# An encoder block on one core: casts of the inverse operands moved ahead in the gates stage, projection stores one step later

## The chip, the cores and the metric

The kernel runs on one core of a Trainium2 chip. The metric is the device time of one execution in microseconds (us); less is better. The engines of a core work side by side, each through its own queue of instructions in the order in which they were written into it: PE (matrix products; its weight loads are listed as PEld), DVE (vector), ACT (scalar and activation), POOL, and SP, which here only issues DMA transfers. An instruction that waits holds up everything behind it on its engine.

## The reference

One layer of a bidirectional encoder block on x of 2048 x 1024 float32. Cut to what matters here:

```
proj = rms_norm(x) @ w_in                                  # 2048 x 3600
cv   = short_conv3(proj[:, :2560])                         # q, k, hv, hx1, hx2
q, k = silu(cv[q]), silu(cv[k]) / sqrt(128);  v, o = proj  # o through a sigmoid
h_m  = mlstm(q, k, v, gates) + flipped mlstm
z    = hx1 * two_sided_fft_conv(hv, filters 0)
z    = hx2 * two_sided_fft_conv(z,  filters 1)
x    = x + rms_norm(concat(norm(h_m * o), norm(z)) @ w_out)
x    = x + rms_norm(square(relu(rms_norm(x) @ w1)) @ w2)
```

The convolution by FFT over 4096 points is done as matrix products in two stages each way: a first forward stage, a second forward stage whose spectrum is multiplied by the filter's, a second inverse stage and a first inverse stage.

## The kernel before

Products in higher precision are made of three: an operand is split into a high part (a cast by `act.copy`, line 166) and a low part (a subtraction, line 169), and `mm3` (lines 154 to 161) multiplies low by high, high by low and high by high into one bank.

The kernel goes through these stages: normalise x; the filters' spectra; the convolution operator `hyena`; the mLSTM; output projection; MLP. The input projection is no stage of its own. It is a generator, `project`, whose pieces `drive` (line 217) lays between those of the filters and of `hyena`: each `yield` of either names a cost, and the projection gets a next piece whenever the cost of the other side is ahead. First come the `convolved` columns (20 tiles of 128 columns, each in four blocks of 512 rows): a block has three pieces, in which `block` makes the products, `centre` and `sides` the width-3 convolution, `turn` the transposes of an earlier block (for all but q and k), `gated` the Silu (for q and k), and `stored` copies the transposes out of their bank (line 626) and stores them by two DMAs of POOL's queue (line 630), or stores q and k by SP's. `ahead` prepares the next column tile's weights: a product on POOL, a cast on ACT, a subtraction on DVE. Then comes `values_project`: four groups of about 260 columns in the order 3, 0, 1, 2, 16 tiles of 128 rows each, in two half steps of 12 products. `outputs` writes a tile from its bank to half of a buffer `vst` (lines 706 and 708; the sigmoid is the o gate), and after the second tile of a pair `stored` issues one store by SP to the tensor `vo`. There are two `vst` buffers and four banks.

From the start of `hyena` the order of all queues is the order in which the code is written out (`manual_schedule`), so a line that is moved moves in every queue.

`hyena` (line 1005) has the first forward stage of hv (16 turns), the second stages with filter 0 (a loop over 32 values of j), then **the gates stage** (lines 1156 to 1190) and the second stages with filter 1. The gates stage has 17 turns h. A turn makes the first inverse products `py` of row tile h from two operands, multiplies them by the gate tile (line 1181) to z, splits z, and makes from z of turn h - 1 the first forward products of the second convolution: `first` (line 1043), two times three products into banks of their own with a `yield` behind each, and then a copy of the first bank by ACT (line 1051), of the second by DVE (line 1052) and a store of the pair by ACT's queue. It splits the two operands of turn h + 1 (`operand`, line 1163: high part on ACT, low part of the first on POOL and of the second on DVE) and issues the three loads of turn h + 2. High parts have four buffers, raw tiles six, z and its low part four between them, products three banks.

Of the kernel before, what the change touches and what calls it, by code (L numbers as in the profile page):

```python
# [8 lines left out]
F32 = mybir.dt.float32  # L9
# [138 lines left out]
class Builder:  # L148
# [410 lines left out]
    def convolved(self, cts, then):  # L559

        wk, hn, cw = self.pw, self.hn, self.cw
        pe, dve, act, pool = self.pe, self.dve, self.act, self.pool
        n = 4 * len(cts)
        fetched, weights, pts, ys, sts = {}, {}, {}, {}, {}

        def ahead(c, step):

            if c >= len(cts):
                next(then)
                return  # L570
            fetch, chunk, m = self.in_weights(128 * cts[c], 128)
            if step == 0:
                fetched[c] = [fetch(q) for q in range(m)]
            else:
                weights.setdefault(c, []).append(chunk(fetched[c][step - 1]))

        def of(i):
            return cts[i // 4], i % 4

        def block(i, ks):  # L580
            ct, b = of(i)
            if ks[0] == 0:
                pts[i] = self.pp.tile([128, 512], F32, tag="pp", name="pt")
            for k in ks:
                self.mm3(pts[i], self.row_block(weights[i // 4], k), (hn[b][0][:, k, :], hn[b][1][:, k, :]), k == 0, k == 7)

        def centre(i):
            ct, b = of(i)
            yc = ys[i] = wk.tile([128, 512], F32, tag="yc", name="yc", bufs=4)
            act.activation(yc, pts[i], AF.Identity, scale=cw[:, ct, 1:2], bias=cw[:, ct, 3:4])  # L590

        def sides(i):
            (ct, b), pt, yc = of(i), pts[i], ys[i]

            def add(y, at, p, src, w):
                dve.scalar_tensor_tensor(y[:, at], p[:, src], cw[:, ct, w:w + 1], y[:, at], ALU.mult, ALU.add)

            if b > 0:

                add(ys[i - 1], slice(511, 512), pt, slice(0, 1), 2)  # L600
                add(yc, slice(0, 1), pts.pop(i - 1), slice(511, 512), 0)
            add(yc, slice(1, 512), pt, slice(0, 511), 0)
            add(yc, slice(0, 511), pt, slice(1, 512), 2)
            if b == 3:
                pts.pop(i)

        def gated(i):
            if of(i)[0] < 8:
                act.activation(ys[i], ys[i], AF.Silu)

        def turn(i):
            ct, b = of(i)
            if ct < 8:
                return
            pt = sts[i] = self.pp.tile([128, 4, 128], F32, tag="ptt", name="ptt", bufs=1)
            for q in range(4):
                pe.transpose(pt[:, q, :], ys[i][:, 128 * q:128 * q + 128], self.eye)

        def stored(i):
            (ct, b), yc = of(i), ys.pop(i)  # L620
            if ct < 8:
                self.load(self.qk[ct // 4][ct % 4][:, 512 * b:512 * b + 512], yc)
                return
            which, cc = (ct - 8) // 4, 128 * (ct % 4)
            st = wk.tile([128, 520], F32, tag="vst", name="vst")[:, 0:512].rearrange("p (q c) -> p q c", q=4)
            act.copy(st, sts.pop(i))  # L626

            dst = self.vp[which].rearrange("h (b a) c -> (h b) a c", a=32)
            for e in range(2):
                pool.dma_start(dst[:, 8 * b + e:8 * b + 8:2, cc:cc + 128], st[64 * e:64 * e + 64])  # L630

        for step in range(3):
            ahead(0, step)
        for i in range(n + 3):
            live, b = i < n, i % 4
            if live:
                block(i, range(0, 3))
            if 1 <= i <= n:
                centre(i - 1)
            if i >= 3:  # L640
                turn(i - 3)
            if live and b == 1:
                ahead(i // 4 + 1, 0)
            yield 2.04 if live else next(then)
            if live:
                block(i, range(3, 6))
            if 1 <= i <= n:
                sides(i - 1)
            if i >= 3:
                stored(i - 3)  # L650
            if live and b > 1:
                ahead(i // 4 + 1, b - 1)
            yield 2.04 if live else next(then)
            if live:
                block(i, range(6, 8))
            if 2 <= i <= n + 1:
                gated(i - 2)
            yield 1.36 if i < n - 1 else 1.36 * live + next(then)

    def values_project(self):  # L660

        wk, act, dve, N = self.pw, self.act, self.dve, 260
        raws, chunks, pts, sts = {}, {}, {}, {}
# [9 lines left out]
        order = (3, 0, 1, 2)  # L673
# [25 lines left out]
        def outputs(g, t):  # L699
            pt, n = pts.pop((g, t)), width(g)  # L700
            if t % 2 == 0:
                sts[g] = wk.tile([128, 520], F32, tag="vst", name="vst").rearrange("p (u c) -> p u c", u=2)
            st = sts[g][:, t % 2]
            nv = 0 if g > 1 else N - 8 if g == 1 else N
            if nv:
                dve.tensor_copy(st[:, 0:nv], pt[:, 0:nv])
            if nv < n:
                act.activation(st[:, nv:n], pt[:, nv:n], AF.Sigmoid)
            if g == 3:

                for d in range(2):
                    c0 = 8 * d
                    dve.tensor_tensor(self.gin[:, :, 64 * d + (15 - t if d else t):64 * d + 64:16],
                                      pt[:, n + c0:n + c0 + 8].rearrange("p (k h) -> p k h", k=2),
                                      bg[:, c0:c0 + 8].rearrange("p (k h) -> p k h", k=2), ALU.add)

        def stored(g, t):
            if t % 2:
                n = width(g)
                self.load(self.vo[128 * t - 128:128 * t + 128, N * g:N * g + n].rearrange("(u p) c -> p u c", p=128),  # L720
                          sts[g][:, :, 0:n])

        last, steps = None, [(g, t) for g in order for t in range(16)]
        for i, (g, t) in enumerate(steps):
            block(g, t, range(0, 4))
            if last:
                outputs(*last)
            yield 1.4
            block(g, t, range(4, 8))
            if last:  # L730
                stored(*last)
            last = g, t
            yield 1.4
            nxt = steps[min(i + 7, len(steps) - 1)][0]
            if nxt != g and t in (9, 11):
                fetch(nxt, t // 11)
            if nxt != g and t == 15:
                for q in range(2):
                    chunk(nxt, q)
                    fetch(nxt, q + 2)  # L740
                yield 4.0
                for q in range(2, 4):
                    chunk(nxt, q)
            if i >= 18 and i % 2 == 0:
                next(gates, None)
        outputs(*last)
        stored(*last)
        for _ in gates:
            pass
# [255 lines left out]
    def hyena(self, pools):  # L1005
        nc, io, tc, dt = self.nc, self.io, self.tc, self.dt
        pe, dve, act, pool = self.pe, self.dve, self.act, self.pool
        wk, ps = pools
# [8 lines left out]
        def parts(raw, low=None, eng=pool):  # L1017

            hi = wk.tile([128, 512], F32R, tag="hi", name="hi", bufs=4)
            low = raw if low is None else low  # L1020
            self.split(hi, low, raw.bitcast(F32), eng)
            return hi, low
# [17 lines left out]
        def short(dtype=F32):  # L1040
            return wk.tile([128, 512], dtype, tag="z", name="z", bufs=4)
# [26 lines left out]
        for o in range(2):  # L1068
# [94 lines left out]
            def operand(h, r):  # L1163
                if h < 16:
                    y.setdefault(h, []).append(parts(x[h][r], eng=(pool, dve)[r]))
# [7 lines left out]
            for h in range(17):  # L1173
                if h < 16:
                    py = bank("py")
                    for r in range(2):
                        self.mm3(py, s1i[r], y[h][r], r == 0, r == 1)
                    y.pop(h)
                    yield 1.0
                    z = short()  # L1180
                    dve.tensor_tensor(z, py, xg.pop(h).bitcast(F32), ALU.mult)
                operand(h + 1, 0)
                if h < 16:
                    zt[h] = parts(z, short(F32R), dve)
                if h >= 1:
                    for _ in first(1, h - 1, s1, zt.pop(h - 1)):
                        yield 1.0
                operand(h + 1, 1)
                if h + 2 < 16:
                    gate_loads(h + 2)  # L1190

# [626 lines left out]
```

## Time and profile before

| | before |
|---|---|
| median of 3 runs | 2786.06 us (2784.33 to 2790.24) |
| the profiled execution's own time | 2789.98 us |
| its span, first to last instruction | 2787.9 us |
| PE busy in the span | 2617.9 us (94%) |
| DVE, ACT, POOL busy | 1530.7, 1223.3, 1199.6 us |
| mean granted clock of PE | 0.973 |

The profile is one execution. Busy times of engines overlap, and a busy share over the whole span is a mean over stages with different limits. The gates stage lies at about 710 to 830 us of the span; the projection runs beside it, with its last convolved blocks up to about 750 us and group 3 of the values after that. A wait is the idle time of an engine just ahead of an instruction, with what ended it.

### The profile page before, as it was taken

Reading aid. Unit: us, or ns where it says so; the run is one execution under the profiler, and the core shown is the slowest. Engines: PE = TensorE matmul, PEld = TensorE weight load, DVE = VectorE, ACT = ScalarE, POOL = GpSimd, SP = SyncE. Lnnn points to the kernel's source line nnn. Section 1 sums busy time; section 2 is a strip of 40 time slices with the busy share of each in tenths; the row PEclk is TensorE's granted clock in tenths of the full one; section 3 lists DMA queues with packets and bytes.
Section 4 is the critical chain, followed back from the end, with each engine's and each line's share of the span. In section 5 each row is a group of like instructions: output and inputs, shape, how many; then the busy total and the mean of one; then the engine's idle time right before and its main releaser. Section 6 shows DMA issues by size and latency. Waiting matters only on the chain. (4 is left out here: it accounts for less than half of the span.)

```text
span 2787.9 us, 35849 instructions
## 1 busy us (share of the span) xinstructions
PE 2617.9 (94%) x12422; PEld 2140.6 (77%) x12422; DVE 1530.7 (55%) x2593; ACT 1223.3 (44%) x2237; POOL 1199.6 (43%) x946
## 2 busy tenths in 40 slices
PE   6999999999899998888996999989999999999998
PEld 5778877777677888776775788868888888888876
DVE  5676643777436664664443454564445443443478
ACT  6355543655434444543332445455445233232244
POOL 1221124554215542424565877777774251310232
PEclk8999999999999999999998999989999999999999
DMA  6233346565556656955665444464445653444546
GB/s 168 61 99 106 106 138 201 183 194 169 189 192 176 186 164 227 267 187 187 212 214 198 143 159 143 156 223 141 157 159 201 222 181 114 113 144 153 194 152 226
DMA packets 307189, 474.24 MB, mean 170 GB/s; under 512 B 37814, under 2 KB 166198, under 8 KB 305984
## 3 DMA queue, kind: packets, MB, share of 16 engines
q1 hardware_dynamic: 231952, 333.24, 38.4%
q10 hardware_dynamic: 70304, 125.98, 12.1%
q0 software_dynamic: 4752, 12.72, 2.1%
q8 instruction: 99, 1.62, 0.2%
q14 instruction: 82, 0.67, 0.1%
HBM read 297.65 MB, written 174.20 MB: 169 GB/s over the span
## 5 line engine op out<-in xcount | busy, mean ns | idle before, releaser
L166 ACT CAST cb<-m 128x1024 fp32r<-128x1024 f32 (+1 forms) x346 | 281.8, 850 | 446.4 <-PE pm L159 385.7
L169 DVE TENSOR_TENSOR cb<-m,cb 128x1024 fp32r<-128x1024 f32 (+1 forms) x222 | 238.9, 1113 | 300.4 <-ACT cb L166 290.6
L159 PE MATMUL pm<-hm,cb 128*128 128x512 f32 x896 | 354.4, 396 | 15.0 <-issue 8.3
L160 PE MATMUL pm<-hm,cb 128*128 128x512 f32 x896 | 353.8, 395 | 13.3 <-POOL hm L169 9.6
L161 PE MATMUL pm<-hm,cb 128*128 128x512 f32 x896 | 352.4, 393 | 0.0
L160 PE MATMUL pm<-cb 128*128 128x512 f32 x880 | 343.9, 391 | 6.4 <-DVE cb L169 6.4
L159 PE MATMUL pm<-cb 128*128 128x512 f32 x880 | 342.7, 390 | 1.0 <-DVE cb L169 1.0
L161 PE MATMUL pm<-cb 128*128 128x512 f32 x880 | 343.1, 390 | 0.0
L169 POOL TENSOR_TENSOR cb<-m,cb 128x1024 fp32r<-128x1024 f32 x124 | 270.4, 2193 | 53.4 <-ACT cb L166 53.4
L1539 DVE TENSOR_TENSOR m<-pm,m 128x512 f32<-128x512 f32 x224 | 154.0, 690 | 243.3 <-PE pm L161 232.5
L159 PE MATMUL pt<-hn,w 128*128 128x512 f32 x640 | 270.9, 423 | 1.0 <-ACT hn L486 0.9
L169 POOL TENSOR_TENSOR raw<-raw,hi 128x512 fp32r<-128x512 f32 x160 | 205.4, 1296 | 129.5 <-ACT hi L166 118.3
L160 PE MATMUL pt<-hn,w 128*128 128x512 f32 x640 | 254.9, 398 | 0.3 <-DVE hn L487 0.2
L161 PE MATMUL pt<-hn,w 128*128 128x512 f32 x640 | 253.6, 396 | 0.0
L159 PEld LDWEIGHTS pm<-hm,cb 128*128 128x128 f32 x896 | 171.0, 191 | 53.2 <-issue 10.0
L160 PEld LDWEIGHTS pm<-hm,cb 128*128 128x128 f32 x896 | 171.0, 191 | 51.4 <-POOL hm L169 11.3
L160 PEld LDWEIGHTS pm<-cb 128*128 128x128 f32 x880 | 165.6, 188 | 43.8 <-DVE cb L169 9.4
L161 PEld LDWEIGHTS pm<-hm,cb 128*128 128x128 f32 x896 | 171.0, 191 | 35.5
L159 PEld LDWEIGHTS pm<-cb 128*128 128x128 f32 x880 | 165.4, 188 | 35.9 <-ACT junk L1728 1.4
L161 PEld LDWEIGHTS pm<-cb 128*128 128x128 f32 x880 | 165.6, 188 | 34.1
L1543 ACT ACTIVATE m<-m 128x512 f32<-128x512 f32 x128 | 80.5, 630 | 219.6 <-DVE m L1539 211.7
L630 POOL DMA_DIRECT2D vp<-vst x96 | 61.2, 642 | 236.4 <-ACT vst L626 235.1
(323 smaller groups left out, 5699.0 us busy)
## 6 DMA issues: line engine op xcount, KB each, us to landing
ga<-m ACTq DMA_DIRECT2D x96, 512.0 KB, 3.8
m<-ga SPq DMA_DIRECT2D x96, 512.0 KB, 3.7
d<-st ACTq DMA_DIRECT2D x64, 512.0 KB, 3.3
m<-in_w_mlp_in_dram SPq DMA_DIRECT2D x62, 512.0 KB, 4.6
m<-in_w_mlp_out_dram SPq DMA_DIRECT2D x114, 256.0 KB, 4.0
raw<-d SPq DMA_DIRECT2D x96, 256.0 KB, 2.8
xt<-in_x_dram SPq DMA_DIRECT2D x32, 512.0 KB, 5.6
dk<-kst SPq DMA_DIRECT2D x32, 512.0 KB, 3.3
```

Of the source, the lines that this page charges most:

```text
L159: pe.matmul(ps, w[1], x[0], start=first, stop=False)
L160: pe.matmul(ps, w[0], x[1], start=False, stop=False)
L161: pe.matmul(ps, w[0], x[0], start=False, stop=last)
L166: self.act.copy(hi, src)
L169: (eng_lo or self.dve).tensor_tensor(lo, src, hi.bitcast(F32), ALU.subtract)
L630: pool.dma_start(dst[:, 8 * b + e:8 * b + 8:2, cc:cc + 128], st[64 * e:64 * e + 64])
L1539: dve.tensor_tensor(dst, a, b, ALU.add)
L1543: act.activation(g, g, AF.Relu)
```

## The change

Three edits, nothing is computed otherwise. In the gates stage the generator `first` is taken by hand: its first three products, a `yield`, then the split of z and the second operand of turn h + 1, then its second three products, a `yield`, and then its copies and its store. So the second operand's split moves from behind the copies and the store to a place ahead of the second three products, and z's split from ahead of the first three products to behind them. In `convolved` the call of `stored` moves from the second piece of a block to the third, behind `ahead` and ahead of `gated`. In `values_project` the store of a pair is issued one step later than the step in which its second tile was written out; the buffers are named by pair for that.

```diff
--- before.py
+++ after.py
@@ -646,13 +646,13 @@
                 block(i, range(3, 6))
             if 1 <= i <= n:
                 sides(i - 1)
-            if i >= 3:
-                stored(i - 3)
             if live and b > 1:
                 ahead(i // 4 + 1, b - 1)
             yield 2.04 if live else next(then)
             if live:
                 block(i, range(6, 8))
+            if i >= 3:
+                stored(i - 3)
             if 2 <= i <= n + 1:
                 gated(i - 2)
             yield 1.36 if i < n - 1 else 1.36 * live + next(then)
@@ -699,8 +699,8 @@
         def outputs(g, t):
             pt, n = pts.pop((g, t)), width(g)
             if t % 2 == 0:
-                sts[g] = wk.tile([128, 520], F32, tag="vst", name="vst").rearrange("p (u c) -> p u c", u=2)
-            st = sts[g][:, t % 2]
+                sts[g, t // 2] = wk.tile([128, 520], F32, tag="vst", name="vst").rearrange("p (u c) -> p u c", u=2)
+            st = sts[g, t // 2][:, t % 2]
             nv = 0 if g > 1 else N - 8 if g == 1 else N
             if nv:
                 dve.tensor_copy(st[:, 0:nv], pt[:, 0:nv])
@@ -718,18 +718,18 @@
             if t % 2:
                 n = width(g)
                 self.load(self.vo[128 * t - 128:128 * t + 128, N * g:N * g + n].rearrange("(u p) c -> p u c", p=128),
-                          sts[g][:, :, 0:n])
-
-        last, steps = None, [(g, t) for g in order for t in range(16)]
+                          sts.pop((g, t // 2))[:, :, 0:n])
+
+        before, last, steps = None, None, [(g, t) for g in order for t in range(16)]
         for i, (g, t) in enumerate(steps):
             block(g, t, range(0, 4))
             if last:
                 outputs(*last)
             yield 1.4
             block(g, t, range(4, 8))
-            if last:
-                stored(*last)
-            last = g, t
+            if before:
+                stored(*before)
+            before, last = last, (g, t)
             yield 1.4
             nxt = steps[min(i + 7, len(steps) - 1)][0]
             if nxt != g and t in (9, 11):
@@ -744,6 +744,7 @@
             if i >= 18 and i % 2 == 0:
                 next(gates, None)
         outputs(*last)
+        stored(*before)
         stored(*last)
         for _ in gates:
             pass
@@ -1180,12 +1181,17 @@
                     z = short()
                     dve.tensor_tensor(z, py, xg.pop(h).bitcast(F32), ALU.mult)
                 operand(h + 1, 0)
+                if h >= 1:
+                    f = first(1, h - 1, s1, zt.pop(h - 1))
+                    next(f)
+                    yield 1.0
                 if h < 16:
                     zt[h] = parts(z, short(F32R), dve)
+                operand(h + 1, 1)
                 if h >= 1:
-                    for _ in first(1, h - 1, s1, zt.pop(h - 1)):
-                        yield 1.0
-                operand(h + 1, 1)
+                    next(f)
+                    yield 1.0
+                    next(f, None)
                 if h + 2 < 16:
                     gate_loads(h + 2)
 
```

## Rows read from the trace of the kernel before

**Rows 1.** Stretches: us, busy PE, PEld, DVE, ACT, POOL, clock, DMA share, GB/s.

```profile
490.00:700.00 210.00, 209.02 (x846) 158.56 (x845) 162.02 (x264) 117.18 (x226) 111.43 (x110) 1.00 0.58 184
709.00:755.00 46.00, 37.44 (x140) 27.49 (x138) 25.56 (x41) 17.43 (x30) 12.22 (x10) 0.89 0.52 177
755.00:823.00 68.00, 60.23 (x355) 50.75 (x355) 28.59 (x59) 29.26 (x52) 12.63 (x10) 0.97 0.60 201
```

**Rows 2.** Groups, 709 to 823 us: busy us, mean ns, idle us before, releasers.

```profile
L166 ACT CAST hi<-raw 128x512 fp32r<-128x512 f32 x29 | 17.6, 615 | 34.5 <-DVE st L1052 22.3 <-DMA raw<-d 8.8 <-ACT st L1051 2.0
...
L169 DVE TENSOR_TENSOR z<-z,hi 128x512 fp32r<-128x512 f32 x15 | 12.7, 848 | 14.3 <-ACT hi L166 14.3
```

**Rows 3.** Time order, one turn: start us, us, instruction, idle before and its releaser.

```profile
784.43 0.69 DVE L1052 COPY st<-p 128x512 f32<-128x512 f32 x1 [0.69 <-PE p L161]
...
785.21 0.33 ACTq L234 DMA_DIRECT2D d<-st  x1
...
785.32 0.19 PEld L160 LDWEIGHTS pt<-w,hn 128*128 128x128 f32 x1
...
785.44 0.19 PEld L161 LDWEIGHTS pt<-w,hn 128*128 128x128 f32 x1
...
785.58 0.62 ACT L166 CAST hi<-raw 128x512 fp32r<-128x512 f32 x1 [1.26 <-DVE st L1052]
...
785.67 0.19 PEld L160 LDWEIGHTS py<-raw,c 128*128 128x128 f32 x1
...
785.90 0.19 PEld L161 LDWEIGHTS py<-hi,c 128*128 128x128 f32 x1
...
786.23 0.69 DVE L169 TENSOR_TENSOR raw<-raw,hi 128x512 fp32r<-128x512 f32 x1 [1.11 <-ACT hi L166]
...
786.98 0.19 PEld L160 LDWEIGHTS py<-raw,c 128*128 128x128 f32 x1 [0.54 <-DVE raw L169]
...
787.09 0.19 PEld L161 LDWEIGHTS py<-hi,c 128*128 128x128 f32 x1
...
787.75 0.69 DVE L1181 TENSOR_TENSOR z<-py,raw 128x512 f32<-128x512 f32 x1 [0.67 <-PE py L161]
```

**Rows 4.** Waits of PE's weight loads, 709 to 755 us: total, times, longest.

```profile
PEld py L159 <- ACT hi L166: 8.9, 5, 5.4
PEld py L160 <- DVE raw L169: 2.1, 4, 0.6
PEld py L160 <- POOL raw L169: 2.0, 2, 1.2
```

**Rows 5.** The same waits, 755 to 823 us.

```profile
PEld py L159 <- ACT hi L166: 8.1, 9, 2.6
PEld py L160 <- DVE raw L169: 5.4, 10, 0.5
```

**Rows 6.** Time order: the two longest pauses of PE's loads.

```profile
748.20 0.29 PEld L159 LDWEIGHTS py<-hi,c 128*128 128x128 f32 x1 [5.41 <-ACT hi L166]
...
772.44 0.19 PEld L159 LDWEIGHTS py<-hi,c 128*128 128x128 f32 x1 [2.56 <-ACT hi L166]
```

**Rows 7.** Stretches around these two pauses, columns as in rows 1.

```profile
747.50:756.00 8.50, 7.00 (x24) 5.47 (x24) 4.43 (x8) 2.59 (x5) 1.27 (x1) 0.65 0.38 123
769.40:779.50 10.10, 7.75 (x38) 6.44 (x38) 4.42 (x9) 4.05 (x9) 1.29 (x1) 0.83 0.74 259
```

**Rows 8.** Time order: a low part on POOL and one on DVE.

```profile
725.89 1.27 POOL L169 TENSOR_TENSOR raw<-raw,hi 128x512 fp32r<-128x512 f32 x1 [8.92 <-ACT hi L166]
...
726.37 1.35 DVE L169 TENSOR_TENSOR z<-z,hi 128x512 fp32r<-128x512 f32 x1 [2.63 <-ACT hi L166]
```

**Rows 9.** Waits of SP's DMA queue, 700 to 840 us: total, times, longest.

```profile
SPq L231 <- ACT vst L708: 30.9, 6, 11.2
```

**Rows 10.** Transfers of the value tensor vo, from its view by tile.

```profile
DMA to landing us min/median/max: 3.2/3.7/7.6
```

**Rows 11.** Time order: a transpose of the convolved columns.

```profile
406.85 0.65 PE L617 MATMUL ptt<-eye,yc 128*128 128x128 f32 x4 [1.94 <-ACT vst L626]
```

## The prediction

> **What bounds the kernel now.** The table of stretches comes first: in the spectra ahead of the gates stage the matmul engine PE is busy for 209.02 of 210 us, but in the two halves of the gates stage for 37.44 of 46 us and 60.23 of 68 us, and the granted clock falls there to 0.89 and 0.97 [rows 1]. Only a stretch in which PE isn't full can give time back, and the place of the change is one. The second view is the table of groups within that stage: ACT sat idle for 34.5 us ahead of the operands' casts, 22.3 of them until the copy of line 1052 on DVE was done [rows 2]. The third is one turn in order of time [rows 3]. There the second operand is cast at 785.58 after 1.26 us of waiting, because in ACT's queue it stands behind the store of the pair, and that store waits for DVE's copy of the second product of the forward stage. The low part follows on DVE at 786.23, and the weight load that needs it comes at 786.98, 0.54 us late. The chain goes from PE's last forward product through a copy, a cast and a subtraction back to PE, which has only the first half of the inverse product to put beside it.
>
> **What the chain costs.** In the first half of the stage PE's loads of the inverse product waited 8.9 us for casts, 2.1 us for DVE's low parts and 2.0 us for POOL's [rows 4]; in the second half 8.1 and 5.4 us [rows 5]. The second half has ten turns, and in each of them the wait is for the second operand.
>
> **Part 1, the second operand's cast goes ahead of the forward copies.** Nothing is added; per turn two casts and two subtractions change place. In the order written out, a turn is: inverse products, projection work, z and first operand, (before: z's split,) first forward products, work, (after: z's split and second operand,) second forward products, work, copies and store, (before: second operand). The second operand so moves ahead by a third of a turn and is no longer behind the store. When it can be ready, from the first load of its turn's inverse products: the last of six loads, 0.23 us apart (785.67 to 785.90), begins at 1.15; z starts 0.66 behind the last load (787.09 to 787.75) and takes 0.69, so 2.5; z's cast follows, its low part starts 0.65 behind that (785.58 to 786.23) and takes 0.69, so 3.85; the second operand's cast of 0.615 has been hidden beside it, and its own low part takes 0.69, so about 4.6 us [rows 2, 3]. When PE needs it: six loads of 0.23, three of them for each of two forward products and for the first half of the next inverse product, and two pieces of projection work of 12 loads of 0.12 us (785.32 to 785.44), together 1.4 + 2.1 + 2.9 = 6.4 us [rows 3]. So 1.8 us are left over, which also hide a sigmoid or a weight cast that stands ahead of it. If that cover were gone, a turn would pay what it pays now, 13.5 / 10 = 1.35 us.
>
> I take the second half's waits as gone: 8.1 + 5.4 = 13.5 us, less 19 ordinary spaces of 0.04 us between loads (0.23 apart, 0.19 long [rows 3]), **12.7 us**. This holds even where the pause was longest, 2.56 us at 772.44 [rows 6]: there Silu and the sigmoid with their table loads stand ahead of the cast, but now run while PE still has forward products and projection work.
>
> In the first half I take only part. The 2.0 us for POOL are the first operand's, which is not moved; casts in the stage waited 8.8 us for their loads [rows 2], and where the first operand's load sets the pace, an earlier second operand only lengthens the wait for the first. Of the other 8.9 + 2.1 = 11.0 us, 5.41 is one pause that ended at 748.20 [rows 6], in a turn whose last piece of work has no matmul. After the change that cast still stands behind a weight cast that needs POOL, and it passes only four things of about 0.6 us (second weight cast, centre, copy, DVE's copy, by the cast's 0.615 [rows 2]). So **2.4 us** of 11.0; bounds 0 and 11.0, or 13.0 with POOL's.
>
> **The clock.** Around the longest pauses the granted clock was 0.65 for 8.5 us and 0.83 for 10.1 us [rows 7]. The two levels are 1.2 and 2.4 GHz, so 0.83 means 34% of 10.1 us at the lower one: 3.4 us for work of 1.7. The pause before it goes, so I count **1.7 us**. The pause at 748.20 gets shorter but stays; its 0.7 x 8.5 / 2 = 3.0 us stand in the range only.
>
> **Part 2, z's split moves back by a third of a turn.** Its user is the forward product of the next turn, behind six inverse loads and a piece of work, so 0; without that cover its cast and low part would cost 1.3 us a turn. What follows it in ACT's and DVE's queues is the second operand, counted above. ACT isn't the bound (29.26 of 68 us [rows 1]).
>
> **A collision.** One low part of z took 1.35 us because POOL's low part had begun 0.48 us before it [rows 8]; undisturbed such a part takes 0.69 [rows 3], the mean of z's group is 0.848 [rows 2]. A collision costs 0.66 us, and the 1.8 us left over hide it: I take 0; the bound is 14 turns x 0.66 = 9.2 us. The Trainium skill, page "SBUF — State Buffer", section "Who interferes with whom", says that a VectorE instruction with both inputs in SBUF and a GpSimd instruction that reads SBUF shut each other out, the later one waiting for the whole of the earlier. By that rule the trace agrees: the 1.35 us end about one undisturbed length after POOL's end.
>
> **Part 3, the stores.** The value store of a pair of tiles goes one step back in SP's queue, past the three loads of one turn (four in the second filter). SP stood 30.9 us in six waits for the sigmoid that fills the store, with gate loads behind it [rows 9]; these should nearly go. No pause of PE in the second half is for a load, so I take 0; a first operand that comes in time is inside the bound of 2.0 us. Against it: two buffers hold the pairs, and the next writer but one comes two half steps behind the store instead of four. Transfers to and from that tensor landed after 3.7 us in the median, at most 7.6 [rows 10]; two half steps are 2.9 us when PE works on the projection alone, 5 to 6 us beside the other work. ACT or DVE may wait 1 us here and there; PE has four banks of projection output to run ahead into, so 0. In the convolved columns the copy, POOL's two DMA issues and SP's store also go back by one piece of work, past a weight product on POOL. One output bank takes the transposes, and the next transposes need this copy; it cost 1.94 us once, when ACT was late [rows 11]. PE is full there and a block lasts far longer than a copy, so 0; the bound is a loss of 48 copies x 0.6 = 29 us.
>
> **Sum.** 12.7 + 2.4 + 1.7 = 16.8, about 17 us. The profiled execution took 2789.98 us, 2.1 more than its span of 2787.9 and 3.9 more than the median of 2786.06. So 2773 for such an execution, and **2769** for the median.
>
> **Rivals.** *The loads take over* (2780): with PE faster, the first operands and their loads, which waited 8.8 us already [rows 2], end the same pauses; only the long ones shrink and some 6 us remain. For it: the first half. Against: SP is freed of the stores' waits. *The low parts collide* (2778): z's and the second operand's subtraction follow each other when POOL's runs; 9.2 us come back on PE's path and 17 - 9 = 8 remain. For it: [rows 8]. Against: POOL's part begins earlier in the turn. The page named above gives this mechanism. *It doesn't do what it says* (2785): the cast needs one of four buffers of high parts; if the one that it is given is freed only by a forward product, it waits nearly as late as before, and 1 us is gained. Against: the inverse products of the turn free two. *Slower* (2793): the value stores' two buffers. Some 24 pairs belong to the last three column groups; at 1 us each on PE's path 24 us are lost, 7 more than is won. It is slower from (17 + 5.6) / 24 = 0.94 us a pair. For it: a landing of 7.6 us [rows 10]. Against: ACT and DVE are half idle and four banks lie between.
>
> **Chances.** Forecast 0.60, loads 0.15, collisions 0.07, no effect 0.11, slower 0.07. Within 0.2% (5.6 us) is about what a measurement of this kernel can't tell from no change; a fifth of the loads' case falls there: faster 0.79, same 0.14, slower 0.07. The best case is all waits and all clock: 12.7 + 13.0 + 1.7 + 3.0, some 30 us, 2756. The other end takes in loads and collisions: 2781. The forecast's own range is 2760 to 2776.
>
> **What will show it.** After: in the stage's second half no wait of PE's loads for a cast or DVE and PE busy for 98%; the stage some 17 us shorter; the operands' casts no longer idle until line 1052; SP's wait for the sigmoid below 10 us; the clock in that half above 0.97. The rest of the kernel keeps its length. What would make it wrong: waits for POOL or loads at the same places, waits of ACT or DVE for value stores that show on PE, or a projection stretch ahead of 700 us that gets longer.

## The result, and the profile after

The changed kernel took 2767.56 us (median of 4 runs, 2765.81 to 2769.69), the kernel before 2785.19 us on the same chip (4 runs): ratio 0.9938, 95% interval 0.9924 to 0.9951, 17.6 us less. Measured once more on another chip it was 0.9944 (0.9932 to 0.9957), 16.1 us less. The forecast was 2769, 16.8 us less. The profiled execution took 2769.69 us with a span of 2767.9.

The stretches after the change, with the columns of [rows 1]:

```profile
490.00:700.00 210.00, 210.00 (x852) 159.84 (x851) 160.73 (x264) 115.36 (x221) 109.57 (x108) 1.00 0.59 187
700.00:755.00 55.00, 47.50 (x200) 37.08 (x199) 29.25 (x47) 24.09 (x43) 14.93 (x12) 0.91 0.57 198
755.00:806.00 51.00, 51.00 (x329) 46.46 (x328) 25.78 (x54) 24.75 (x46) 11.39 (x9) 1.00 0.76 247
```

The second half of the gates stage is full, at a granted clock of 1.00; the first half is much as it was: 86% busy at 0.91, where the same 55 us of the kernel before were 84% busy (46.44 us) at 0.91. The waits of PE's weight loads between 700 and 755 us (total, times, longest), which answer to [rows 4]; between 755 and 806 us, which answers to [rows 5], the view is empty:

```profile
PEld py L159 <- ACT hi L166: 6.8, 4, 2.4
PEld py L160 <- POOL raw L169: 2.3, 2, 1.2
PEld py L160 <- DVE raw L169: 1.7, 3, 0.8
```

The groups of operand splits between 709 and 806 us, as in [rows 2] (line 1052 of before is 1053 now):

```profile
L166 ACT CAST hi<-raw 128x512 fp32r<-128x512 f32 x29 | 17.8, 615 | 18.6 <-DMA d<-st 6.9 <-DMA raw<-d 6.6 <-DVE st L1053 2.4
L169 DVE TENSOR_TENSOR z<-z,hi 128x512 fp32r<-128x512 f32 x15 | 12.3, 820 | 11.9 <-ACT hi L166 11.9
```

The casts' idle time until DVE's copy fell from 22.3 to 2.4 us. What is left ends with DMA transfers.

To place the gain, the stage is cut at its own work. The 1st, 6th and 16th z of the kernel before, in order of time:

```profile
711.54 0.69 DVE L1181 TENSOR_TENSOR z<-py,raw 128x512 f32<-128x512 f32 x1 [0.91 <-PE py L161]
...
750.18 0.69 DVE L1181 TENSOR_TENSOR z<-py,raw 128x512 f32<-128x512 f32 x1 [1.31 <-PE py L161]
...
822.70 0.69 DVE L1181 TENSOR_TENSOR z<-py,raw 128x512 f32<-128x512 f32 x1 [0.81 <-PE py L161]
```

and of the changed kernel:

```profile
708.91 0.69 DVE L1182 TENSOR_TENSOR z<-py,raw 128x512 f32<-128x512 f32 x1 [0.71 <-PE py L161]
...
745.85 0.68 DVE L1182 TENSOR_TENSOR z<-py,raw 128x512 f32<-128x512 f32 x1
...
805.00 0.69 DVE L1182 TENSOR_TENSOR z<-py,raw 128x512 f32<-128x512 f32 x1 [2.13 <-PE py L161]
```

The first five turns went from 38.6 to 36.9 us, the last ten from 72.5 to 59.2: 1.7 and 13.4 us, 15.1 in the stage from first to last z (111.2 to 96.1). The other 4.9 us between the two spans lie ahead of it (2.6) and behind it (2.3). They are not shown to be the change's: two kernels of this study with the same work up to the first z, the one with four more subtractions and the one with z's move alone, begin it 4.5 us apart, at 708.1 and 712.6 us.

### The profile page after: what moved, and what is told of

The parts are those of the page before. It is cut to its first block, busy times and chain, and to the rows that moved or that the text cites. A ratio compares the mean times of both kernels' runs of the same rounds, so it can differ in the third digit from the quotient of the medians.

```text
span 2767.9 us, 35869 instructions
## 1 busy us (share of the span) xinstructions
PE 2605.8 (94%) x12422; PEld 2138.0 (77%) x12422; DVE 1520.8 (55%) x2593; ACT 1221.5 (44%) x2237; POOL 1202.9 (43%) x946
## 5 line engine op out<-in xcount | busy, mean ns | idle before, releaser
L160 PE MATMUL pm<-hm,cb 128*128 128x512 f32 x896 | 354.5, 396 | 13.4 <-POOL hm L169 9.9
L596 DVE SCALAR_TENSOR_TENSOR yc<-pt,cw,yc 128x511 f32<-128x511 f32 (+1 forms) x280 | 135.0, 515 | 50.5 <-ACT yc L590 48.5
```

The lines of the kernel that those rows point to most:

```text
L160: pe.matmul(ps, w[0], x[1], start=False, stop=False)
```

## The experiments

All of them in one table: the ratio to the kernel before on the same chip, with its interval, and the time from the first to the last z in the profiled execution. That last figure is the sharper of the two where only the gates stage is in question; it was 96.1 and 96.3 us in two executions of the changed kernel. For every other kernel it comes from one execution.

| kernel | median, us | ratio [95%] | first to last z, us |
|---|---|---|---|
| before | 2785 to 2786 | 1 | 111.2 |
| changed, measured again | 2769.97 | 0.9944 [0.9932, 0.9957] | 96.3 |
| gates stage alone | 2771.67 | 0.9949 [0.9937, 0.9961] | 95.5 |
| stores alone | 2783.47 | 0.9990 [0.9981, 0.9999] | 110.2 |
| without the convolved stores' move | 2772.91 | 0.9951 [0.9938, 0.9963] | 95.2 |
| second operand moved, z not | 2772.95 | 0.9954 [0.9942, 0.9966] | 97.8 |
| z moved, second operand not | 2782.13 | 0.9984 [0.9974, 0.9993] | 107.4 |
| two more subtractions a turn | 2785.51 | 0.9999 [0.9990, 1.0008] | 110.7 |
| four more subtractions a turn | 2807.95 | 1.0078 [1.0064, 1.0092] | 130.6 |
| weight fetches later | 2763.61 | 0.9922 [0.9908, 0.9936] | 88.2 |
| first low part on DVE | 2764.47 | 0.9926 [0.9913, 0.9938] | 92.0 |
| fetches later, second operand ahead of z | 2760.27 | 0.9911 [0.9896, 0.9926] | 86.7 |
| the same, first low part on DVE | 2759.50 | 0.9906 [0.9893, 0.9920] | 85.8 |

**The change taken apart.** Two kernels split the gates stage from the stores.

> The kernel before with the new order of the gates stage alone; both kinds of stores stay where they were. My theory: the order of the two operands' casts is the whole gain. In the stage's second half no wait of PE's loads for a cast or a DVE low part is left, the stage is about 15 us shorter, and the time is 2768 to 2771, within 2 us of the changed kernel; SP's wait for the sigmoid stays near 31 us and costs nothing. Rival: the gate loads behind SP's 31 us are what holds the first operand, so the new order needs the later stores: then waits for loads take the place of those for casts, half of the gain is left, and the time is 2775 to 2779.

> The kernel before with both kinds of stores one step later; the gates stage keeps its old order. My theory: SP's wait for the sigmoid falls from 31 us to below 10, PE keeps its waits for the second operand (about 13 us in the stage's second half), and the time stays within 2 us of the kernel before, 2783 to 2787. Rival: earlier gate loads free the first operands, 3 to 6 us are won, 2779 to 2782. Second rival: the later stores cost something by their two buffers or the one bank of transposes (one wait of 6.0 us for that bank stands in the changed kernel near 406 us), 2788 or more.

The new order alone gives all that the stage gains (15.6 us here, 15.1 in the changed kernel) and 14.2 us (10.9 to 17.5) of the time. Its second half shows no wait of PE's loads, though SP still stood 22.5 us for the sigmoid (the text above expected 31):

```profile
SPq L231 <- ACT vst L708: 22.5, 6, 6.4
```

So the gate loads behind SP's waits were not what PE waited for there. With the stores alone this wait falls from 30.9 us [rows 9] to 8.7, and PE waits as before:

```profile
PEld py L159 <- ACT hi L166: 17.8, 16, 5.4
PEld py L160 <- DVE raw L169: 8.1, 15, 0.6
PEld py L160 <- POOL raw L169: 2.1, 2, 1.2
```

The time moved by 2.8 us (0.3 to 5.3), of which the stage shows 0.9; where the rest would lie isn't settled. So the theory, within 2 us of the kernel before, held by the median, and neither rival came. A third kernel keeps the gates stage and the value stores and puts the convolved stores back.

> The changed kernel with the stores of the convolved columns back where they were; the new order of the gates stage and the later value stores stay. My theory: the move of these stores is worth nothing, 2766 to 2769; the wait of 6.0 us for the one bank of transposes near 406 us goes, but it stands in a place that is made good later or comes once. Rival: that wait is a loss that the changed kernel pays, and the time is 2761 to 2764. Second rival: the move is worth something where PE is full, and undoing it costs 2 us or more, 2770 to 2774.

Its median lies in the range of the second rival, 3 to 5 us above the changed kernel's two medians, but those were taken on other chips, and the intervals of the ratios overlap: this move isn't told from nothing. It does have a price in one place of the changed kernel, a wait of PE between 400 and 490 us that was 1.94 us before [rows 11] and is 2.3 without the move:

```profile
PE ptt L617 <- ACT vst L626: 6.0, 1, 6.0
```

The price is made good: at 490 to 700 us PE is busy for 210.00 of 210 us with the move and for 209.02 without it; between 400 and 490 us four waits of PE for split operands and a copy, 3.0 us in all without the move, are gone with it; and the first z comes no later.

**The two moves inside the gates stage.**

```diff
                 operand(h + 1, 0)
+                if h < 16:
+                    zt[h] = parts(z, short(F32R), dve)
                 if h >= 1:
                     f = first(1, h - 1, s1, zt.pop(h - 1))
                     next(f)
                     yield 1.0
-                if h < 16:
-                    zt[h] = parts(z, short(F32R), dve)
                 operand(h + 1, 1)
```

> The changed kernel with the split of z put back ahead of the first forward products; only the second operand is moved ahead of the copies. My theory: this move is the gain and that of z is worth 0, so the time is that of the changed kernel, 2766 to 2769, and the stage's second half shows no wait of PE's loads for casts. Rival: with z's split so early, z's low part and POOL's low part of the first operand run at one time more often, and 3 us or more come back, 2771 or more.

The stage is 1.7 us longer than with both moves, so the second operand, with the stores, carries 13.4 of the 15.1 us. The time agrees with the rival, but not its reason: 1.45 of the 1.7 us lie in the one turn with Silu and its table loads (7.08 instead of 5.63 us from z to z). Low parts do meet more often there, as the rival said: the mean of z's low part over the 16 turns is 980 ns instead of 812. But outside the Silu turn all this costs the stage 0.3 us. The reverse kernel has z's split where the change puts it, and `operand(h + 1, 1)` behind the store again.

> The changed kernel with the second operand put back to the end of the turn; only z's split is moved, behind the first forward products. My theory: the second operand's cast again stands behind the store of the pair, so the waits of the second half are back (8 us for casts and 5 us for DVE, about 1.35 us in a turn) and the time is 2781 to 2785. Rival: it is z's split, a cast and a low part out of the way of the turn's start, that makes room: then the time is 2774 or less.

Its waits of the second half, 750 to 825 us, are nearly all there again:

```profile
PEld py L159 <- ACT hi L166: 6.5, 8, 1.6
PEld py L160 <- DVE raw L169: 5.4, 10, 0.5
```

It gains 4.5 us (1.9 to 7.2); the stage gives 3.7, of which the stores alone gave 0.9. So z's move is worth about 2 us in the stage (1.7 by the kernel above, 2.8 by this one), where the sum had 0. It lies in the Silu turn and the one behind it again: there the wait for the second operand's cast is 1.08 us instead of the 2.54 of the kernel with the stores alone, and the granted clock between 755 and 823 us 1.00 instead of 0.97. The traces show why the wait is shorter. With the stores alone, Silu's table load stands behind z's cast, which waits for z:

```profile
764.07 0.69 DVE L1182 TENSOR_TENSOR z<-py,raw 128x512 f32<-128x512 f32 x1 [0.82 <-PE py L161]
...
764.85 0.62 ACT L166 CAST hi<-z 128x512 fp32r<-128x512 f32 x1 [1.80 <-DVE z L1182]
765.48 1.28 ACT L609 ACT_TABLE_LOAD   x1
```

With z's split moved, the piece of projection work that holds Silu comes ahead of z's cast in ACT's queue. The table load begins 1.0 us ahead of z instead of 1.4 us behind z's start, and the second operand's cast, behind it on ACT, is done sooner:

```profile
764.76 1.28 ACT L609 ACT_TABLE_LOAD   x1
...
765.77 0.69 DVE L1182 TENSOR_TENSOR z<-py,raw 128x512 f32<-128x512 f32 x1 [0.82 <-PE py L161]
```

**How much cover the second operand has.** z's low part is computed again, into the same tile, two or four times more in each turn:

```diff
                     zt[h] = parts(z, short(F32R), dve)
+                    for _ in range(2):        # 4 in the second kernel
+                        dve.tensor_tensor(zt[h][1], z, zt[h][0].bitcast(F32), ALU.subtract)
```

> The changed kernel with z's low part computed three times instead of once in each turn of the gates stage (the same subtraction again, into the same tile), so that the second operand's low part starts two subtractions, about 1.4 us, later. In the trace of the changed kernel that low part ends about 1.5 us ahead of the weight load that needs it (the sum said 1.8). My theory, that this is the whole cover: the two are just hidden, 2766 to 2771, few waits of PE's loads for DVE. Rival, that DVE's queue is already the limit and the copies of the forward stage and z come later too: 16 turns of 0.7 us or more are lost, 2778 or more.

> The changed kernel with z's low part computed five times instead of once in each turn of the gates stage; the second operand's low part starts about 2.8 us later. My theory of the cover: 2.8 less 1.5 us are not hidden, about 1.25 us in each of 10 to 15 turns, so 12 to 19 us are lost and the time is 2780 to 2787, with waits of PE's loads of the inverse product for DVE in nearly every turn. Rival: PE has far more work queued than the sum counts, and the time stays below 2772. Second rival: z itself comes late as well and each of the four subtractions costs its full 0.69 us in 16 turns, 44 us, 2810.

My theory fell for both. With two, the time is in the range of the rival (2778 or more), but the loss is not spread over 16 turns as the rival had it: it lies in the first five turns and around the Silu turn, and in an ordinary turn the theory holds. The changed kernel, in order of time (the low part ends at 789.90, its load is at 791.41, so 1.5 us are left):

```profile
788.35 0.62 ACT L166 CAST hi<-raw 128x512 fp32r<-128x512 f32 x1
788.47 0.82 DVE L169 TENSOR_TENSOR z<-z,hi 128x512 fp32r<-128x512 f32 x1 [0.74 <-ACT hi L166]
...
789.22 0.68 DVE L169 TENSOR_TENSOR raw<-raw,hi 128x512 fp32r<-128x512 f32 x1
...
791.41 0.19 PEld L160 LDWEIGHTS py<-raw,c 128*128 128x128 f32 x1
```

and the same with two more subtractions, which end 0.3 us before the load at 795.81, with no wait (where an ordinary turn of the second half has one, it is at most 0.43 us):

```profile
793.50 1.42 DVE L1191 TENSOR_TENSOR z<-z,hi 128x512 fp32r<-128x512 f32 x2
...
794.84 0.68 DVE L169 TENSOR_TENSOR raw<-raw,hi 128x512 fp32r<-128x512 f32 x1
...
795.81 0.19 PEld L160 LDWEIGHTS py<-raw,c 128*128 128x128 f32 x1
```

But the turn with Silu has no such cover. Its two table loads of 1.28 us stand ahead of both casts, and in the changed kernel its low part was ready only 0.2 us before its load (762.98 for 763.20). With two more subtractions:

```profile
771.21 1.28 ACT L708 ACT_TABLE_LOAD   x1
...
773.28 0.62 ACT L166 CAST hi<-raw 128x512 fp32r<-128x512 f32 x1
...
776.21 0.29 PEld L160 LDWEIGHTS py<-raw,c 128*128 128x128 f32 x1 [2.08 <-DVE raw L169]
```

The granted clock from 770 to 782 us is then 0.73. And in the first five turns, where PE already waits for the first operand, there is none: they take 45.0 us instead of 36.9, 8.0 us more for five times 1.4. The last ten turns take 65.7 instead of 59.2, most of it around the Silu turn. With four, the ten take 78.1 us, 18.9 more (the 1.25 us a turn of the theory would be 12.5), the time passes the theory's upper end of 2787, and the first five 52.5. The 38 us in all are near the second rival's 44, but it is not z that is waited for: 28.9 us of PE's waits are for the second operand's low part.

**What is left in the first half.** In the changed kernel SP fetches the third piece of the value weights in the step in which the first is prepared, and its buffer is free only when DVE has made the low part of that first piece:

```profile
717.11 0.69 DVE L169 TENSOR_TENSOR w<-wf,w 128x520 fp32r<-128x520 f32 x1
717.82 0.38 SPq L231 DMA_DIRECT2D wf<-in_w_in_dram  x1
718.30 0.90 SPq L231 DMA_DIRECT2D raw<-d  x2
...
722.66 0.62 ACT L166 CAST hi<-raw 128x512 fp32r<-128x512 f32 x1 [6.87 <-DMA d<-st]
...
723.33 0.19 PEld L159 LDWEIGHTS py<-hi,c 128*128 128x128 f32 x1 [1.66 <-ACT hi L166]
```

The loads `raw<-d` of the gates stage stand behind that fetch in SP's queue. The experiment moves only the fetch:

```diff
             chunk(3, q)
-            fetch(3, q + 2)
             yield 0.0
+            fetch(3, q + 2)
```

> The changed kernel, and the third and fourth fetch of the first value columns' weights are issued one step later, so that SP doesn't hold the gate loads of the turn while the fetch waits for the low part of a weight on DVE. My theory: the 10.8 us that PE's loads of the inverse product still wait in the first half of the gates stage are first operands whose loads are behind that fetch; SP's wait for DVE's weights falls from 26 us to below 10, PE's waits to about 4 us, and the time is 2759 to 2764. Rival: the operands are late for their own buffers or landing, not for SP, and nothing moves: 2766 to 2769. Second rival: the weights come too late for the value projection and it is slower, 2770 or more.

Nearly as the theory said: the time is at the upper end of its range, and SP's wait for DVE's weights between 700 and 840 us falls from 25.7 to 10.7 us, not below 10. By the ratios the kernel is 4 to 6 us faster than the changed one, on other chips and with intervals that overlap. The stage is 88.2 us, 7.9 less; between 700 and 755 us PE is busy for 52.15 us at a clock of 0.97, and of 10.8 us of waits of the inverse product's loads 4.6 are left:

```profile
PEld py L159 <- ACT hi L166: 2.7, 2, 2.4
PEld py L160 <- DVE raw L169: 1.5, 2, 0.9
PEld py L160 <- POOL raw L169: 0.4, 1, 0.4
```

**Whether low parts collide.**

```diff
-                    y.setdefault(h, []).append(parts(x[h][r], eng=(pool, dve)[r]))
+                    y.setdefault(h, []).append(parts(x[h][r], eng=dve))
```

> The changed kernel once more, on the chip of the next three, so that these can be held against it. Expected 2765 to 2770, ratio 0.993 to 0.995.

> The changed kernel with the first operand's low part on DVE instead of POOL in the gates stage, so that no low part of DVE can meet one of POOL there (the product of the weights stays on POOL). My theory: meetings cost nothing where the low part has 1.5 us to spare, the 0.69 us more on DVE takes part of that, and the two waits of 1.2 us for POOL go: within 2.5 us of the changed kernel. Rival, that the low parts' meeting is what holds the rest: z's mean falls from 829 to 690 ns and the time falls by 4 us or more. Second rival, from the run with two more subtractions: DVE's queue has cover only in the second half, so that 0.69 us more are paid in the first half, 3 to 6 us slower.

The time fell by 5.5 us by the medians (the stage by 4.4), as the first rival said, and z's mean over the 16 turns fell from 811 to 734 ns: 15 of the 16 now take 0.69 us, one takes 1.40. The waits speak against the meetings as the cause. Those of PE's loads between 700 and 755 us:

```profile
PEld py L159 <- ACT hi L166: 4.7, 5, 1.7
PEld py L160 <- DVE raw L169: 3.1, 6, 0.6
```

Waits for DVE went up from 1.7 to 3.1 us, though its low parts are shorter; those for POOL (2.3) are gone, and those for casts went from 6.8 to 4.7. In the changed kernel one of these casts comes late through POOL:

```profile
740.66 2.06 POOL L543 TENSOR_TENSOR wf<-wf,nw 128x520 f32<-128x520 f32 x2
...
741.75 0.62 ACT L166 CAST w<-wf 128x520 fp32r<-128x520 f32 x1 [1.86 <-POOL wf L543]
742.28 0.61 ACT L166 CAST hi<-z 128x512 fp32r<-128x512 f32 x1
...
742.79 0.61 ACT L166 CAST hi<-raw 128x512 fp32r<-128x512 f32 x1
...
743.46 0.29 PEld L159 LDWEIGHTS py<-hi,c 128*128 128x128 f32 x1 [2.41 <-ACT hi L166]
```

POOL's product of the weights stands behind POOL's low part of the first operand, the weight's cast waits for the product, and both operands' casts queue behind it. With that low part on DVE, PE's wait at this place is 1.06 us. From z to z, 2.9 of the 4.4 us lie in this turn and 1.2 in an earlier one, in which PE had waited 1.17 us for POOL's low part. This account is read from one execution of each kernel; a kernel that moves only the weights' product wasn't run.

**A better version.** On top of the later fetches, the second operand goes ahead of z's split as well.

> The kernel with the later weight fetches, and the second operand's cast and low part stand ahead of z's split instead of behind it. My theory: what PE's loads still wait for in the gates stage is one turn whose cast is behind a weight cast that waits for POOL (2.4 and 0.9 us); an order of two casts changes little of that, so the time is within 2 us of the kernel with the later fetches, 2761 to 2764. Rival: the cover of the second operand, 1.5 us, is what is short, and 1.4 us more of it wins 3 us or more, below 2761. Second rival: z's forward products then wait for z.

> The same, and the first operand's low part is on DVE instead of POOL. My theory: with the second operand ahead of z on DVE the 0.69 us more are covered, the last wait for POOL's low part goes, and POOL is free for the weights' products: 1 to 3 us faster than the same kernel with that low part on POOL, 2758 to 2762. Rival: DVE is late for the second operand as it was with two more subtractions, and it is 3 us or more slower.

The stage is 86.7 and 85.8 us: 1.5 and 0.8 us less with each step. The first time, 2760.27, lies below the theory's range and in that of the rival (3 us or more from the second operand's place), by medians of different chips; the stage shows half of that, the intervals overlap, and it isn't settled. The second lies in its theory's range, but 0.8 us on the same chip isn't told from nothing. Both are faster than the kernel before by about 26 us, and than the changed kernel on the same chip by about 10.

## Why the prediction was right

**The second operand, 12.7 us, with 1.7 of clock.** The ten turns of the second half gave 13.4 of 14.4, by a slightly other split: 11.2 with the second operand's move and the stores, the rest with z's. What the 13.4 are made of is seen from the 6th to the 16th z, before and after (columns of [rows 1]):

```profile
750.18:822.70 72.52, 64.75 (x373) 54.65 (x373) 31.80 (x65) 30.40 (x54) 12.63 (x10) 0.95 0.58 194
745.85:805.00 59.15, 59.15 (x373) 53.89 (x373) 30.89 (x65) 30.46 (x55) 13.96 (x11) 0.98 0.75 248
```

PE had been idle for 7.8 us, which are gone, though its loads had waited 13.5 us [rows 5]; the other 5.6 us are the same 373 products taking less busy time, at a granted clock of 0.98 instead of 0.95. By the prediction's own way of pricing the clock that is 0.05 of 72.5 less 0.02 of 59.2, an estimate of 2.4 us where the sum had 1.7. About 11 are left for the waits, so 12.7 was some 1.7 too high. The two errors nearly cancel; what shortened the busy time beyond the clock isn't shown. The signs that were named came: no wait there, PE at 100%, idle time until DVE's copy 22.3 to 2.4 us, SP's wait for the sigmoid 7.5 us, clock 1.00. The stage is 15.1 us shorter, where 17 were forecast.

**Its cover, 1.8 us.** In the ten turns of the second half it was 1.5 to 2.0 us in seven, 3.0 in one, 0.9 in the first and 0.2 in the Silu turn, so the count of loads was right. That it would "also hide a sigmoid or a weight cast" was too easy: in the Silu turn next to nothing was left, and two subtractions more cost what the change had won.

**The first half, 2.4 of 11.0 us.** It gave 1.7, but not at the pause from which the 2.4 were worked out; that the two numbers lie near is luck. The second operand's pause of 5.41 us did shrink, to 2.41 (at 743.46). But in that turn the first operand now waits for its load, where it had not:

```profile
738.74 0.62 ACT L166 CAST hi<-raw 128x512 fp32r<-128x512 f32 x1 [6.58 <-DMA raw<-d]
...
739.41 0.19 PEld L159 LDWEIGHTS py<-hi,c 128*128 128x128 f32 x1 [2.43 <-ACT hi L166]
```

From z to z that turn takes 11.2 us, where it took 11.0; what was won lies in the three turns ahead of it (24.1 to 22.3 us). The reason given for taking only part, that the first operand's load sets the pace and an earlier second operand only lengthens that wait, is just what this turn shows, and the later fetches confirm it: with them the stage lost another 7.9 us, 3.4 of them in this turn. So the rival that the loads take over was true for the first half and for it alone, which is how the sum had it.

**z's split, 0.** Too low by about 2 us, nearly all of them in the Silu turn and the turn behind it. The sum looked at who needs z, and not at what z's cast, waiting for z, held up behind it on ACT.

**Collisions, 0.** Right as to the second operand: low parts still meet, and z's mean falls from 811 to 734 ns with POOL's part gone, but PE's waits for DVE don't fall with it; nor does the stage lengthen by more than 0.3 us outside the Silu turn where z's earlier split makes more of them meet (980 ns). The Trainium skill, page "SBUF — State Buffer", section "Who interferes with whom", has a VectorE instruction with both inputs in SBUF and a GpSimd instruction that reads SBUF contend for one shared port, and the later one wait. The trace agrees: without POOL's part 15 of 16 of z's low parts take 0.69 us. What POOL's low part cost was, as far as these traces show, a wait of PE for it and time in POOL's own queue ahead of the weights' product; the sum did not look at that queue.

**The stores, 0.** SP's waits went, and the stage didn't need it (95.5 us without). The two value buffers do wait longer: between 753 and 1060 us the sigmoid stood 13.0 us and DVE's copy 7.4 us for a store, where before it was one wait of 5.6 us of the sigmoid. Only a part of this is the later stores': with the stores alone it is one wait of 6.7 us of DVE's copy, and the sigmoid's 13.4 us are there with the gates stage alone. PE shows no wait for those buffers, so they were not on its path, and the rival with the slower end didn't come. In all the stores are worth 0 to 5 us.

## What to carry to other kernels

A wait of the tensor engine for an operand is taken away by asking what stands ahead of that operand's cast in its queue, not by making the cast cheaper; here a copy and a store that waited for the engine's own products stood there, and nothing had to be added. Work out how long before its use the moved work is ready, and do so for the worst turn, the one with table loads or weights in the queue, because the mean turn's spare time is not there. When one half of a stage has become full, look in the other half for what a DMA queue holds up: a fetch that waits for a buffer stops every load behind it.

## What the runs showed that was not expected

A wait on the profile need not be a loss: 6.0 us for one bank at about 406 us left the first z no later, and other waits there and in the next 210 us fell away (a cost below the 4.5 us by which that start differs between kernels with the same work wouldn't be seen). And a small delay costs more than its waits: two subtractions of 0.69 us in each turn lengthened the stage by 14.6 us, while the waits of the inverse product's loads grew from 10.8 to 22.1 us; the granted clock of the 53.5 us up to the first sigmoid's tile was 0.84 and that of the 57.2 us behind it 0.94, against 0.89 and 1.00 in the changed kernel.
